# Two more pairs of hidden tiles by seven products, with the weight sums of two pairs made in DRAM

## The chip, the core and the metric

The kernel runs on one core of a Trainium2 chip. The core has five engines with a queue of instructions each: PE (TensorE, matrix products; its weight loads are shown apart as PEld), DVE (VectorE), ACT (ScalarE), POOL (GpSimd) and SP (SyncE, which here only issues transfers). Each engine works its queue in order and waits on semaphores for the others. SBUF holds 128 partitions of working data, PSUM has eight banks of 128x512 float32 for the results of PE, and DRAM holds inputs, output and scratch. The metric is the device time of one execution in microseconds (us). Before the change it was 916.53 us, the median of three runs (915.88 to 916.86).

## What is computed

One layer of a decoder on 512 tokens of width 1024, all in float32: a SwiGLU feed-forward part (FFN), a mixing part (windowed attention next to a state-space scan), a second FFN, each between two RMS norms.

```python
def swiglu(x, w_in, w_out):
    gate, up = jnp.split(x @ w_in, 2, axis=-1)
    return (jax.nn.silu(gate) * up) @ w_out

h = rms_norm(x, ffn1_pre_g[l])
x = x + 0.5 * rms_norm(swiglu(h, ffn1_w_in[l], ffn1_w_out[l]), ffn1_post_g[l])
...
mixed = jnp.concatenate([attn, ssm], axis=-1) @ w_mix_out[l]
x = x + rms_norm(mixed, mix_post_g[l])
h = rms_norm(x, ffn2_pre_g[l])
x = x + 0.5 * rms_norm(swiglu(h, ffn2_w_in[l], ffn2_w_out[l]), ffn2_post_g[l])
```

`w_in` is 1024 x 5632: 22 tiles of 128 columns for the gate and 22 for the up side. The hidden width of 2816 is 22 tiles of 128, counted by f below.

## The kernel before

**Precision.** Every large product is made of three products of a reduced float32 form: an operand is split into a high part (a cast on ACT) and a low part (a subtraction on DVE or POOL), and high x high, high x low and low x high are added in one PSUM bank. `wsplit` (lines 117 and 119) does it for weights, which land in tiles named wraw, wa, wx or wsum and are split into whi and wlo; `split` (lines 163 to 167) does it for activations, named xh and xl, ah and al, bh and bl, tq. All matmuls go through line 144. POOL takes the subtraction where the call says pool=True.

**Order.** The program is written as one sequence and a scheduler puts it into the queues. What is wrapped in `fix` keeps its place in the written order on its engine, and so do all matmuls; the rest is moved about by readiness. Generators ("hooks") hand small pieces of work to the loops of matmuls between two products.

**Standard tiles and pairs.** A tile f of the hidden width takes one product of eight steps for the gate and one for the up side: 2 x 24 matmuls of 512 columns (`products`, the bank is named gu). From some tile on the kernel takes two tiles at once (`pair`), and treats the gate and up sides of the two tiles with the two halves of the inner width (blocks a11, a12, a21, a22) against the four quarters of the activations (b11 to b22) as a 2x2 block product, by Winograd's form of Strassen's scheme: seven products of 24 matmuls with 256 columns, in banks named wx, wy and wq. The price is sums. On the weights' side, per pair, on DVE: c3 = a11 + a21, c2 = c3 + a22, c1 = a21 + a22, c4 = c2 + a12 (line 609). On the activations' side, once: n1, n2, t3, t4. The activations of the pairs are scaled by the norm's reciprocal first (line 533, `scaled`, sixteen instructions of 128x256), then summed and split into seven operands. After the products the gate half is gathered (lines 621 and 638), passed through Silu on ACT (line 639), multiplied with the up half (line 644) and split into ah and al.

**The stages.** First FFN: tiles 0 to 7 standard, then pairs 8 to 20. A `boundary` ends each part: it makes the last output products (yt), adds the residual for half of the tokens at a time (`prep`, lines 317, 319, 166, 167) and starts the next part's first four products step by step behind it (`begin`, the banks are named first). For the second FFN these are tiles 0 and 1. `swiglu_half` then runs tiles 2 to 5 as standard products, with eight transposes of x (`tokens_first`, xt) hooked in between, then the output product of tiles 0 to 5 (`outp(0)`, bank yo), pairs 6, 8 and 10, outp(1), pairs 12, 14 and 16, outp(2), pairs 18 and 20, and `finish`: the last four tiles' output products (yt), the norm and the store. The number of standard tiles is `NSTD = (8, 6)`.

**Buffers.** Weights land in three wraw buffers; a pair's a21 lands in one buffer wa, a22 in two wx, and c1 to c4 take three wsum buffers. A load is issued when its buffer is free, and SP issues in order, so a load that waits holds those behind it.

Of the kernel before, what the change touches and what calls it, by code (L numbers as in the profile page):

```python
# [29 lines left out]
NSTD = (8, 6)  # L30
# [14 lines left out]
class Layer:  # L45
# [30 lines left out]


# [195 lines left out]
    def boundary(self, y, tail, ipost, half, inext, chunks):  # L273
# [40 lines left out]
        def prep(h, k, fix=lambda i: i):  # L314
            t = y(k)[:, hs[h]]
            xk = self.x(k)[:, hs[h]]
            fix(nc.vector.scalar_tensor_tensor(out=t, in0=t, scalar=self.g(ipost, k, half), in1=rr[h],
                                               op0=ALU.mult, op1=ALU.mult))
            fix(nc.vector.tensor_tensor(out=xk, in0=t, in1=xk, op=ALU.add))
            self.split(xh(k)[:, hs[h]], xl(k)[:, hs[h]], xk, self.g(inext, k), fix)  # L320
            self.sq_acc(acc2[:, hs[h]], xk, k == 0, nc.gpsimd)
# [68 lines left out]
    def ffn(self, n, first, scope):  # L390
# [84 lines left out]
        prep = sums(True)  # L475
# [35 lines left out]
    def seven(self, fin, w_in, ig, r, ah, al):  # L511
# [13 lines left out]
        def sums(early=False):  # L525
# [20 lines left out]
            bh, bl = [self.b16(n, F32R) for n in ("bh", "bl")] if early else (None, None)  # L546
            v = lambda t, i: t.rearrange("p (q k) c -> p q (k c)", q=4)[:, i]

            def plain(*ts):
                for t in ts:  # L550
                    i = len(blocks)
                    blocks.append((v(bh, i), v(bl, i)))
                    self.split(*blocks[i], t)

            if early:
                plain(b11)
# [9 lines left out]
            if early:  # L566
                plain(b22, n1)
# [4 lines left out]
            if not early:  # L572
                yield
                bh, bl = [self.b16(n, F32R) for n in ("bh", "bl")]
                plain(b11, b21, b22, n1)
# [11 lines left out]
        def cut(t, pool=False):  # L587
            hi, lo = self.halves(True)
            self.wsplit(t, hi, lo, pool)
            return hi, lo  # L590

        def times(bank, w, xb, first, parted=False):
            for g in range(2):
                for k in range(4):
                    m = slice((4 * g + k) * P, (4 * g + k + 1) * P)
                    st = first and g == 0 and k == 0
                    for i, (wi, xi) in enumerate(((0, 0), (0, 1), (1, 0))):
                        for a, b in ((0, P), (P, HT)) if parted and (g, k, i) == (0, 1, 0) else ((0, HT),):
                            self.mm(bank[:, g * HT + a:g * HT + b], lhsT=w[wi][:, m], rhs=xb[xi][:, k * HT + a:k * HT + b],
                                    start=st and i == 0, stop=g == 1 and k == 3 and i == 2, skip_group_check=True)  # L600
# [6 lines left out]
        def pair(f, lead=False, late=False):  # L607
            (b11, b21, b22, n1), (n2, t3, t4) = blocks, tq
            add = lambda x, z, t: V.tensor_tensor(out=t, in0=x, in1=z, op=ALU.add)
            p2 = lambda t: t.rearrange("p (f c) -> p f c", f=2)  # L610
            half = lambda t, h: t[:, :, h * HT:(h + 1) * HT]
            gt = p2(gp())
            X = self.bank("wx")
            a11 = block(f, 0, 0)
            times(X, cut(a11), b11, True, lead)
            s1 = keep(X)
            a12 = block(f, 0, 1)
            h12 = cut(a12, True)
            Y = self.bank("wy")
            times(Y, h12, b21, True)  # L620
            V.tensor_tensor(out=half(gt, 0), in0=p2(Y), in1=p2(s1), op=ALU.add)
            a21, a22 = block(f, 1, 0), block(f, 1, 1)
            c3 = wsum()
            add(a11, a21, c3)
            c2 = wsum()
            add(c3, a22, c2)
            times(X, cut(c2), n2, False)
            s2 = keep(X)
            c1 = wsum()
            add(a21, a22, c1)  # L630
            Q = self.bank("wq")
            times(Q, cut(c1), n1, True)
            q = keep(Q)
            times(X, cut(c3), t3, False)
# [3 lines left out]
            V.tensor_tensor(out=half(gt, 1), in0=p2(Q), in1=p2(s2), op=ALU.add)
            nc.scalar.activation(out=gt, in_=gt, func=AF.Silu)
            times(X, cut(a22, True), t4, False)  # L640
# [9 lines left out]
        return sums, pair  # L650

    def swiglu_half(self, first, scope):

# [3 lines left out]
        fin = scope.enter_context(self.tc.tile_pool(name="fin", bufs=1))  # L657
        hook = self.tokens_first(fin)
        self.pad(fin, 192)
        o0, _, r, late = first  # L660
        ah, al = self.ktiles("ah", F32R), self.ktiles("al", F32R)
        o = {f: o0[2 * f:2 * f + 2] for f in range(len(o0) // 2)}
        step = lambda: next(hook, None)
        hooks = {(2, 0): {1: step, 3: step, 5: late[0], 7: step}, (2, 1): {0: step, 2: late[1], 4: step, 6: step},
                 (3, 0): {1: step, 3: step, 5: step}, (3, 1): {1: step}}

        def products(f):
            o[f] = []
            for i, c in enumerate((f, NF + f)):
                into = [fin.tile([P, 1024], F32R, name="tq", tag=f"tq2{j}") for j in range(2)] if (f, i) == (2, 0) else None  # L670
                w = self.load(w_in[c], (KD, P), into, pool=i == 1)
                b = self.bank("gu")
                self.mmk(b, w, self.xh, self.xl, hooks=hooks.get((f, i), {}))
                o[f].append(b)

        def hidden(f):
# [3 lines left out]
            V.tensor_tensor(out=ut, in0=o[f][1], in1=r, op=ALU.mult)  # L680
            V.tensor_tensor(out=ut, in0=ut, in1=gt, op=ALU.mult)
            self.split(ah(f % RING), al(f % RING), ut)

        def outp(i):
            f0, nf = FLAST[i]
            for d in range(2):
                b4 = [self.bank("yo") for _ in range(4)]
                for k in range(nf):
# [12 lines left out]
        sums, pair = self.seven(fin, w_in, 4, r, ah, al)  # L701
        for f in range(NSTD[1]):
            if f >= len(o0) // 2:
                products(f)
            if f == 2:
                hidden(0)
                hidden(1)
            if f >= 2:
                hidden(f)
            if f == 3:  # L710
                for _ in hook:
                    pass
                rest = sums()
                for _ in range(7):
                    next(rest)
        next(rest)
# [6 lines left out]
        for f in range(NSTD[1], NF, 2):  # L723
            pair(f, f in (NSTD[1], 12, 18), f == NF - 2)
# [13 lines left out]
        self.finish(fin, y, lambda k: (ah((NF - NT + k) % RING), al((NF - NT + k) % RING)))  # L738

    def finish(self, fin, y, tail):  # L740
# [29 lines left out]
        def gather(b, i):  # L770
            yi = at(y, b, i)
            fx(V.tensor_tensor(out=yi, in0=o[b, i], in1=yi, op=ALU.add))
            fx(nc.scalar.activation(out=self.tmp("sq")[:, :yi.shape[-1]], in_=yi, func=AF.Square,
                                    accum_out=sums[:, b, i:i + 1]))

        def gain(b, i):
# [3 lines left out]
            fx(V.tensor_tensor(out=yg[b, i], in0=at(y, b, i), in1=self.gt[d][:, sl], op=ALU.mult))  # L780
# [644 lines left out]
    def run(self, parts="fmg"):  # L1425
# [4 lines left out]
        first = self.start(chunks, ipre)  # L1430
        for p, q in zip(parts, parts[1:] + " "):
            with ExitStack() as scope:
# [6 lines left out]
                if p != "g":  # L1439
                    first = self.boundary(*out, *post[p], *nxt[q])  # L1440
# [67 lines left out]
```

## Time and profile before

| what | value |
|---|---|
| median of 3 runs | 916.53 us |
| the profiled execution, its own time | 916.19 us |
| its span, first to last instruction | 914.2 us |
| granted clock of PE | 0.998 |
| busy: PE, DVE, ACT, POOL | 898.9, 656.0, 442.0, 217.5 us |
| standard tiles 2 to 5 of the second FFN | 584.72 to 634.36 us of the span |
| outp(0) | 634.36 to 667.16 us |
| pairs 6, 8 and 10 | 667.16 to 724.43 us |
| pairs 8, 10 and 12 of the first FFN | 150.32 to 207.59 us |

A row of the timeline has the start, the length, the engine, the line, the operation, what it writes and reads, how many instructions were merged, and in brackets the idle time before it and what ended it. The end of a matmul is modelled and overlaps the next one's start, so the pace of PE is read from starts. A row of the chain of waits has a start and the time by which that piece took the chain further.

### The profile page before, as it was taken

How to read it: one execution, taken by the hardware profiler on the slowest of the kernel's cores; microseconds unless marked ns; L12 is line 12 of the kernel's file. 1: busy time of each engine (PE TensorE's matmuls, PEld its weight loads, DVE VectorE, ACT ScalarE, POOL GpSimd, SP SyncE). 2: the span in 40 equal slices, each digit the busy share in tenths (PEclk: the TensorE clock that was granted, in tenths of full speed). 3: DMA queues.
4: the chain of work that ended last, by engine and by line, in shares of the span. 5: the costliest groups of instructions: out<-in, count | busy, mean ns of one | idle time of the engine just before them, and what ended most of it. 6: DMA issues, size and time to landing. Idle time of an engine off the chain costs nothing.

```text
span 914.2 us, 15367 instructions
## 1 busy us (share of the span) xinstructions
PE 898.9 (98%) x6169; PEld 801.4 (88%) x6169; DVE 656.0 (72%) x1071; ACT 442.0 (48%) x685; POOL 217.5 (24%) x127
## 2 busy tenths in 40 slices
PE   9999999999999999999999999999999999999996
PEld 7787789998999989978777889888899989998995
DVE  6999786755678666758898567898368557855756
ACT  6263763553355543525745654573355514541542
POOL 0423301322123134500000025523222222221321
PEclk9999999999999999999999999999999999999999
DMA  8223662334231262283321452145222422332222
GB/s 277 94 70 115 196 248 76 107 102 137 77 119 61 68 194 86 92 221 109 116 70 51 153 167 71 29 179 180 97 93 99 133 92 93 116 116 92 92 93 92
DMA packets 47734, 106.81 MB, mean 117 GB/s; under 512 B 7824, under 2 KB 11152, under 8 KB 47120
## 3 DMA queue, kind: packets, MB, share of 16 engines
q1 hardware_dynamic: 46080, 102.21, 34.5%
q10 hardware_dynamic: 1584, 3.63, 1.1%
q8 instruction: 48, 0.79, 0.3%
q14 instruction: 22, 0.18, 0.1%
HBM read 96.13 MB, written 9.70 MB: 116 GB/s over the span
## 4 chain that ended last, share of the span: by engine, by line
PE 79%; DVE 6%; issue 2%; DMA 2%; ACT 1%; POOLq 0%; POOL 0%; DVEq 0%; SPq 0%; ACTq 0%
PE yo L144 21%; PE wx L144 18%; PE wq L144 9%; PE yt L144 6%; PE wy L144 4%; PE gu L144 4%; PE prj L144 4%; PE first L144 3%; PE prv L144 2%; PE mo L144 2%; PE ys L144 1%; PE st L144 1%; DMA w1d<-w1s 1%; PE pt L1098 1%; PE sc L144 1%
## 5 line engine op out<-in xcount | busy, mean ns | idle before, releaser
L117 ACT CAST whi<-wraw 128x1024 fp32r<-128x1024 f32 (+5 forms) x128 | 124.0, 976 | 160.3 <-PE yo L144 65.5
L119 POOL TENSOR_TENSOR wlo<-wraw,whi 128x1024 fp32r<-128x1024 f32 (+1 forms) x41 | 109.2, 2666 | 297.6 <-ACT whi L117 290.3
L119 DVE TENSOR_TENSOR wlo<-wraw,whi 128x1024 fp32r<-128x1024 f32 (+5 forms) x87 | 107.4, 1242 | 75.7 <-ACT whi L117 75.6
L144 PE MATMUL wx<-tq,whi 128*128 128x256 f32 x720 | 124.7, 276 | 0.0
L144 PEld LDWEIGHTS wx<-tq,whi 128*128 128x128 f32 x720 | 108.3, 188 | 0.0
L119 DVE TENSOR_TENSOR wlo<-wsum,whi 128x1024 fp32r<-128x1024 f32 x60 | 73.6, 1227 | 46.5 <-ACT whi L117 46.4
L117 ACT CAST whi<-wsum 128x1024 fp32r<-128x1024 f32 x60 | 63.0, 1050 | 81.8 <-PE yo L144 28.1
L144 PE MATMUL wx<-tq,wlo 128*128 128x256 f32 x360 | 99.4, 276 | 0.0
L119 POOL TENSOR_TENSOR wlo<-wx,whi 128x1024 fp32r<-128x1024 f32 x15 | 41.5, 2764 | 176.3 <-ACT whi L117 128.5
L144 PEld LDWEIGHTS wx<-tq,wlo 128*128 128x128 f32 x360 | 67.6, 188 | 0.0
L144 PE MATMUL gu<-xh,whi 128*128 128x512 f32 x168 | 67.2, 400 | 0.0
L144 PE MATMUL gu<-xh,wlo 128*128 128x512 f32 x168 | 65.7, 391 | 1.1 <-POOL wlo L119 1.1
L144 PE MATMUL wq<-bh,whi 128*128 128x256 f32 x240 | 66.2, 276 | 0.0
L144 PE MATMUL wq<-bl,whi 128*128 128x256 f32 x240 | 66.2, 276 | 0.0
L144 PE MATMUL wq<-bh,wlo 128*128 128x256 f32 x240 | 66.2, 276 | 0.0
L144 PE MATMUL gu<-xl,whi 128*128 128x512 f32 x168 | 65.5, 390 | 0.0
L144 PE MATMUL yo<-ah,whi 128*128 128x512 f32 x144 | 56.3, 391 | 0.0
L144 PE MATMUL yo<-al,whi 128*128 128x512 f32 x144 | 56.1, 389 | 0.0
L144 PE MATMUL yo<-wlo,ah 128*128 128x512 f32 x144 | 56.0, 389 | 0.0
L144 PE MATMUL yo<-whi,ah 128*128 128x512 f32 x144 | 56.0, 389 | 0.0
L144 PE MATMUL yo<-ah,wlo 128*128 128x512 f32 x144 | 56.0, 389 | 0.0
L144 PE MATMUL yo<-whi,al 128*128 128x512 f32 x144 | 56.0, 389 | 0.0
(267 smaller groups left out, 2385.0 us busy)
## 6 DMA issues: line engine op xcount, KB each, us to landing
wraw<-w1i SPq DMA_DIRECT2D x28, 512.0 KB, 3.7
wraw<-w2i SPq DMA_DIRECT2D x28, 512.0 KB, 3.6
wraw<-w2o SPq DMA_DIRECT2D x18, 512.0 KB, 3.7
wraw<-wmi SPq DMA_DIRECT2D x12, 512.0 KB, 4.1
wraw<-w1o SPq DMA_DIRECT2D x8, 512.0 KB, 4.2
wa<-w2i SPq DMA_DIRECT2D x8, 512.0 KB, 3.7
wx<-w2i SPq DMA_DIRECT2D x8, 512.0 KB, 4.0
wa<-w1i SPq DMA_DIRECT2D x7, 512.0 KB, 3.6
```

The lines of the kernel that those rows point to most:

```text
L117: fix(self.nc.scalar.copy(out=hi, in_=raw))
L119: fix(eng.tensor_tensor(out=lo, in0=raw, in1=hi.bitcast(F32), op=ALU.subtract))
L144: i = self.nc.tensor.matmul(*a, **k)
L1098: self.fix(nc.tensor.transpose(b[i][:, o:o + P], sc[:, c:c + P], self.ident))
```

## The change

1. `NSTD` becomes (8, 2): in the second FFN tiles 2 to 5 are the pairs 2 and 4. There are no standard products there any more but those of tiles 0 and 1 in the boundary.
2. For pairs 2 and 4 the sums c1 to c4 are made in DRAM scratch (`block_sums`): each by a plain transfer from SP and an accumulating transfer from POOL, 16 transfers in all, issued step by step between the products of the first FFN's pairs 8, 10, 12 and 14. Pairs 2 and 4 load the finished sums (`whole`). The other pairs still make theirs on DVE; a21 now lands in a wsum buffer and c1 is written over it.
3. The activations' operands of the second FFN's pairs are not scaled by the norm's reciprocal r any more. The parts xh and xl of the boundary serve directly as three of the seven operands; n1, n2, t3 and t4 are made from an unscaled copy gx, which ACT writes in `prep` and from which DVE makes n1 and n2 in the boundary's second half (`wide_sums`). In return the gate half of each pair is multiplied with r before Silu (one DVE instruction of 128x1024 per pair), and the up side's factor is put into `finish` through r4.
4. The first two weight blocks of pair 2 are loaded and split in the boundary (tile ahead). In pair 2 the order on ACT, DVE and SP is pinned.
5. The eight transposes of x move from the standard products to the steps of outp(0). The boundary makes the norm's reciprocal for 512 tokens at once, after pair 2's first product, instead of twice for 256.

```diff
-NSTD = (8, 6)
+NSTD = (8, 2)
+EARLY = (2, 4)
...
+    def block_sums(self):
+        nc, w = self.nc, self.a["w2i"]
+        src = lambda f, up, kh: w[f + NF * up:f + NF * up + 2, :, kh * S:(kh + 1) * S].rearrange("f p c -> p f c")
+        t = self.csum = {(f, c): self.dr.tile([P, 2, S], F32, name=f"c{c}_{f}") for f in EARLY for c in (3, 1, 2, 4)}
+        copy = lambda o, i: self.dma(out=o, in_=i)
+        plus = lambda o, i: self.fix(nc.gpsimd.dma_start(out=o, in_=i, accum_op=ALU.add))
+        make = {"3": lambda f: copy(t[f, 3], src(f, 0, 0)), "+3": lambda f: plus(t[f, 3], src(f, 1, 0)),
+                "1": lambda f: copy(t[f, 1], src(f, 1, 0)), "+1": lambda f: plus(t[f, 1], src(f, 1, 1)),
+                "2": lambda f: copy(t[f, 2], t[f, 3]), "+2": lambda f: plus(t[f, 2], src(f, 1, 1)),
+                "4": lambda f: copy(t[f, 4], t[f, 2]), "+4": lambda f: plus(t[f, 4], src(f, 0, 1))}
+        order = "3a 1a 3b +3a 1b +1a - +3b 2a +1b - 2b +2a - - +2b 4a - +4a - 4b - - +4b"
...
@@ boundary, prep
             self.split(xh(k)[:, hs[h]], xl(k)[:, hs[h]], xk, self.g(inext, k), fix)
+            if wide:
+                fix(nc.scalar.activation(out=t, in_=xk, func=AF.Copy, scale=self.g(inext, k)))
             self.sq_acc(acc2[:, hs[h]], xk, k == 0, nc.gpsimd)
...
             begin(1, k)
-            if k == 3:
+            if wide and k:
+                wide(k - 1)
+            if not wide and k == 3:
                 pre[0][0](fixp=fx)
...
@@ pair
+            if ahead:
+                split = lambda t: cut(t, pin=True)
+                h2, h1 = split(whole(f, 2)), split(whole(f, 1))
+                times(X, ahead[0], blocks[0], True)
+                s1 = keep(X)
+                then(0)
+                then(1)
+                h3 = split(whole(f, 3))
+                Y = self.bank("wy")
+                times(Y, ahead[1], blocks[1], True)
+                then(2)
+                then(3)
+                gate(0, Y, s1)
+                then(4)
+                h4 = split(whole(f, 4))
+                times(X, h2, tq[0], False, True)
+                s2 = keep(X)
+                then(5)
+                h22 = split(block(f, 1, 1))
...
             gate(1, Q, s2)
+            if csum:
+                V.tensor_tensor(out=gt, in0=gt, in1=r.unsqueeze(1).to_broadcast([P, 2, S]), op=ALU.mult)
             nc.scalar.activation(out=gt, in_=gt, func=AF.Silu)
...
+    def wide_sums(self, gx):
...
+            hi, lo = (room[:, kh, i] for i in range(2))
+            self.wsplit(raw, hi, lo)
...
+            if k < 4:
+                V.tensor_tensor(out=h(k, 0), in0=h(k, 0), in1=h(k, 1), op=ALU.subtract)
+            else:
+                V.scalar_tensor_tensor(out=self.n2[:, (k - 4) * HT:(k - 3) * HT], in0=h(k - 4, 0), scalar=-1.0, in1=h(k, 1),
+                                       op0=ALU.mult, op1=ALU.subtract)
...
@@ swiglu_half
+        pair(2, hooks={0: lambda: late[0](fix=self.fix, fixp=self.fix), 1: third, 2: late[1], 3: lambda: put_in(1, 0, 1), 4: fourth,
+                       5: lambda: put_in(2, 1, 0)}, ahead=self.first)
+        hidden(0)
+        hidden(1)
...
+        pair(4)
```

The change moves instructions at three places on which the prediction rests.

**POOL in the first FFN's pairs.** Here wlo<-wx is the low part of a pair's a22 and wlo<-wraw that of the next pair's a12. Before:

```order
L119 TENSOR_TENSOR wlo<-wraw,whi 128x1024
L119 TENSOR_TENSOR wlo<-wx,whi 128x1024
L119 TENSOR_TENSOR wlo<-wraw,whi 128x1024
L119 TENSOR_TENSOR wlo<-wx,whi 128x1024
L119 TENSOR_TENSOR wlo<-wraw,whi 128x1024
```

With the change (c_2 and c_4 are the DRAM sums of pairs 2 and 4):

```order
L139 TENSOR_TENSOR wlo<-wraw,whi 128x1024
L87 DMA c_2_1577<-w2i 256x1x512
L87 DMA c_2_1578<-w2i 256x1x512
L139 TENSOR_TENSOR wlo<-wx,whi 128x1024
L139 TENSOR_TENSOR wlo<-wraw,whi 128x1024
L87 DMA c_4_1581<-w2i 256x1x512
L87 DMA c_4_1582<-w2i 256x1x512
L139 TENSOR_TENSOR wlo<-wx,whi 128x1024
L139 TENSOR_TENSOR wlo<-wraw,whi 128x1024
L87 DMA c_2_1579<-w2i 256x1x512
L87 DMA c_4_1583<-w2i 256x1x512
```

Two accumulating transfers stand behind each a12 and ahead of the same pair's a22; the last two, not shown, stand behind pair 14's a12.

**DVE from the boundary's last steps into the second FFN.** Before, the scaling of all quarters (gp and wx from x) and the norm's reciprocal (nv) stand here around the low parts of tile 2's and 3's weights:

```order
L319 TENSOR_TENSOR x<-ymix,x 128x256
L167 SCALAR_TENSOR_TENSOR xl<-x,sm,xh 128x256
L205 TENSOR_SCALAR nv<-st 128x2
L533 SCALAR_TENSOR_TENSOR gp<-x,sm,rs 128x256 x4
L533 SCALAR_TENSOR_TENSOR wx<-x,sm,rs 128x256
L119 TENSOR_TENSOR wlo<-wraw,whi 128x1024
L533 SCALAR_TENSOR_TENSOR wx<-x,sm,rs 128x256 x3
L205 TENSOR_SCALAR nv<-st 128x2
```

With the change:

```order
L339 TENSOR_TENSOR x<-ymix,x 128x256
L756 SCALAR_TENSOR_TENSOR n_5912<-ymix 128x256
L187 SCALAR_TENSOR_TENSOR xl<-x,sm,xh 128x256
L756 SCALAR_TENSOR_TENSOR n_5912<-ymix 128x256
L184 TENSOR_TENSOR tq<-ymix,tq 128x1024
L184 TENSOR_TENSOR tq<-n_5912,tq 128x1024
L139 TENSOR_TENSOR wlo<-wsum,whi 128x1024 x2
L225 TENSOR_SCALAR nv<-st 128x4
L788 TENSOR_TENSOR ymix<-ymix 128x4x256
L139 TENSOR_TENSOR wlo<-wsum,whi 128x1024
```

The scaling is gone; one of the eight steps of n1 and n2 follows each xl, and two operand splits and two weight splits stand ahead of the reciprocal.

**DVE in the last pair.** Before:

```order
L638 TENSOR_TENSOR gp<-wq,kp 128x2x256
L644 SCALAR_TENSOR_TENSOR gp<-kp,gp 128x2x256
L644 SCALAR_TENSOR_TENSOR gp<-wx,gp 128x2x256
L164 TENSOR_TENSOR al<-gp,ah 128x2x256 x2
L772 TENSOR_TENSOR y<-yt,y 128x512
```

With the change:

```order
L651 TENSOR_TENSOR gp<-wq,kp 128x2x256
L719 TENSOR_TENSOR gp<-gp,rs 128x1024
L726 SCALAR_TENSOR_TENSOR gp<-kp,gp 128x2x256
L726 SCALAR_TENSOR_TENSOR gp<-wx,gp 128x2x256
L184 TENSOR_TENSOR al<-gp,ah 128x2x256 x2
L890 TENSOR_TENSOR y<-yt,y 128x512
```

The multiplication with r stands between the gate's gathering and the step that needs Silu's result; the instructions behind it are the same.

More of the change, by code (lines that the diff above doesn't have):

```diff
@@ L551, in plain @@
                     i = len(blocks)
[L552 to L556, printed above, removed]
+                    b = v(bh, i), v(bl, i)
+                    blocks.append([v4(u) for u in b])
+                    self.split(*b, t)
+            plain(b11)
             V.scalar_tensor_tensor(out=n2, in0=n1, scalar=-1.0, in1=b22, op0=ALU.mult, op1=ALU.subtract)
-            if early:
-                plain(b21)
+            plain(b21)
             yield
@@ L571, in sums, with pairs @@
             self.split(*tq[2], t4)
[L572 to L575, printed above, removed]
             yield
+        return sums, self.pairs(w_in, blocks, tq, wsum, gp, (wsum, wx), r, ah, al)
+    def pairs(self, w_in, blocks, tq, wsum, gp, rooms, r, ah, al, csum=None):
+        nc, V = self.nc, self.nc.vector
+        wa, wx = rooms
         def block(f, up, kh):
             if up:
-                t = wx() if kh else more[0].tile([P, 1024], F32, name="wa", tag="wa")
+                t = wx() if kh else wa()
             else:
@@ L605, in keep, with pair @@
             return t
-        def pair(f, lead=False, late=False):
-            (b11, b21, b22, n1), (n2, t3, t4) = blocks, tq
+        def pair(f, lead=False, late=False, hooks={}, ahead=None):
             add = lambda x, z, t: V.tensor_tensor(out=t, in0=x, in1=z, op=ALU.add)
@@ L611, in pair @@
             half = lambda t, h: t[:, :, h * HT:(h + 1) * HT]
+            then = lambda i: hooks[i]() if i in hooks else None if csum else self.more()
+            four = csum and (f, 2) in csum
             gt = p2(gp())
             X = self.bank("wx")
[L614 to L634, printed above, removed]
@@ L639, in pair @@
+            gate(1, Q, s2)
+            if csum:
+                V.tensor_tensor(out=gt, in0=gt, in1=r.unsqueeze(1).to_broadcast([P, 2, S]), op=ALU.mult)
             nc.scalar.activation(out=gt, in_=gt, func=AF.Silu)
-            times(X, cut(a22, True), t4, False)
+            then(6)
+            times(X, h22 if ahead else cut(a22, True), tq[2], False)
             s = f % RING
@@ L699, in outp @@
                         V.tensor_tensor(out=y(b, d), in0=b4[b], in1=y(b, d), op=ALU.add)
[L701 to L716, printed above, removed]
+        blocks[3] = put(3, part(gx, 0, 0))
+        tq[0] = put(0, n2)
+        wsum = lambda: fin.tile([P, 1024], F32, name="wsum", tag="wsum", bufs=3)
+        pair = self.pairs(w_in, blocks, tq, wsum,
+                          lambda: fin.tile([P, 1024], F32, name="gp", tag="gp"), (wsum, lambda: fin.tile([P, 1024], F32, name="wx", tag="wx", bufs=2)), r, ah, al, self.csum)
+        pair(2, hooks={0: lambda: late[0](fix=self.fix, fixp=self.fix), 1: third, 2: late[1], 3: lambda: put_in(1, 0, 1), 4: fourth,
+                       5: lambda: put_in(2, 1, 0)}, ahead=self.first)
+        hidden(0)
+        hidden(1)
         self.gt = [self.acct() for _ in range(2)]
@@ L722, in swiglu_half @@
         outp(0)
[L723 to L724 removed]
+        for _ in hook:
+            pass
+        for f in range(6, NF, 2):
+            pair(f, f in (6, 12, 18), f == NF - 2)
             if f in (10, 16):
```

158 lines of the change are left out of this document (118 added, 40 removed).

## The prediction

> **What bounds the kernel now.** I read the busy times first, then the shares of the chain of waits.
>
> ```profile
> PE 898.9 (98%) x6169; PEld 801.4 (88%) x6169; DVE 656.0 (72%) x1071; ACT 442.0 (48%) x685; POOL 217.5 (24%) x127
> PE 79%; DVE 6%; issue 2%; DMA 2%; ACT 1%; POOLq 0%; POOL 0%; DVEq 0%; SPq 0%; ACTq 0%
> ```
>
> PE is busy for 898.9 of 914.2 us and holds 79% of the chain. An edit pays where it takes matmuls away or ends a wait of PE; freeing DVE pays nothing by itself. The windows of four stages follow (stretch, its length, busy time and count on PE, PEld, DVE, ACT and POOL, granted clock, DMA share, GB/s).
>
> ```profile
> 584.72:634.36 49.64, 48.44 (x234) 40.00 (x233) 46.22 (x54) 27.84 (x38) 19.01 (x7) 1.00 0.46 159
> 634.36:667.16 32.80, 32.80 (x147) 27.18 (x146) 13.69 (x11) 10.94 (x14) 5.50 (x2) 1.00 0.31 98
> 667.16:724.43 57.27, 57.27 (x507) 57.27 (x506) 39.15 (x39) 31.72 (x37) 15.51 (x6) 1.00 0.31 104
> 150.32:207.59 57.27, 57.27 (x506) 57.27 (x506) 38.91 (x39) 31.03 (x37) 14.96 (x6) 1.00 0.30 96
> ```
>
> The first is the stage that is replaced, tiles 2 to 5: PE lacks 1.20 us, DVE is nearly full (46.22 of 49.64). In outp(0), the second, DVE works 13.69 of 32.80. In three pairs of either FFN (57.27, so 19.09 a pair) PE never idles and the clock is 1.00. The first FFN's pairs matter because the new transfers are issued there.
>
> **The matmuls.** Two pieces of the chain of waits give the pace (start, time, engine, tile, line, matmuls).
>
> ```profile
> 605.93 28.60 PE gu L144 x126
> 667.16 2.87 PE wx L144 x25
> 670.03 2.72 PE wy L144 x24
> ```
>
> A matmul of 512 columns takes 28.60 / 126 = 0.2270 us, one of 256 columns 2.72 / 24 = 0.1133. Tiles 2 to 5 are 8 x 24 = 192 of the first: 43.58. Pairs 2 and 4 are 2 x 7 x 24 = 336 of the second: 38.08. Term A is **-5.50**. One matmul of pair 2 is parted in two, as in the 25-row piece above: 2.87 - 2.72 = **+0.15** (term B).
>
> **The wait that goes.** The timeline around 593 us:
>
> ```profile
> 583.95 6.83 DVE L533 SCALAR_TENSOR_TENSOR gp<-x,sm,rs 128x256 f32<-128x256 f32 x4 [2.56 <-ACT rs L215]
> 585.37 5.12 POOL L119 TENSOR_TENSOR wlo<-wraw,whi 128x1024 fp32r<-128x1024 f32 x2
> 592.03 0.40 PE L144 MATMUL gu<-xh,wlo 128*128 128x512 f32 x1
> 593.42 0.15 DVE L205 TENSOR_SCALAR nv<-st 128x2 f32<-128x2 f32 x1
> 593.63 0.66 PE L505 MATMUL xt<-ident,x 128*128 128x128 f32 x4 [1.20 <-DVE nv L205]
> ```
>
> The product of 592.03 should have been followed 0.227 later, at 592.26; the next matmul starts at 593.63, 1.4 late. The releaser nv stood on DVE behind the scaling, whose four instructions took 6.83 us while POOL made two low parts. This scaling and this place of nv are gone. The sum of the stage agrees: 43.58 + eight transposes + st and rp + 1.4. A transpose is 597.32 to 597.68 with a slower start of the next product (next rows), 0.45; 8 x 0.45 = 3.6; what is left of 49.64 for st and rp is 1.06. So term C is **-1.4**, if nothing takes its place.
>
> ```profile
> 597.32 0.60 PE L505 MATMUL xt<-ident,x 128*128 128x128 f32 x4
> 597.68 0.48 PE L144 MATMUL gu<-xh,whi 128*128 128x512 f32 x1
> ```
>
> What could: nv now stands behind two operand splits and two weight splits (about 1.2 us each, 4.8) after the last xl. Its reader, rp, comes in PE's order after pair 2's second product, 2 x 2.72 = 5.44 after the first four products end. The slack is 5.44 - 4.8, some 0.3 after ACT's part between them; the other operands of pair 2 have more. I take 0, bound 0 to +1.2.
>
> **Transposes moved.** The same eight go to outp(0), 3.6 there and 3.6 less here: **0** (term D), bound 0 to +1, since their results must leave PSUM beside yo's; DVE has 19 us free in that stage, ACT 22.
>
> **Boundary, second half.** DVE now also makes one step of n1 or n2 per step of prep.
>
> ```profile
> 572.25 0.47 DVE L167 SCALAR_TENSOR_TENSOR xl<-x,sm,xh 128x256 fp32r<-128x256 f32 x1
> 572.65 0.41 DVE L319 TENSOR_TENSOR x<-ymix,x 128x256 f32<-128x256 f32 x1
> 572.99 0.48 DVE L167 SCALAR_TENSOR_TENSOR xl<-x,sm,xh 128x256 fp32r<-128x256 f32 x1
> 580.84 0.48 DVE L167 SCALAR_TENSOR_TENSOR xl<-x,sm,xh 128x256 fp32r<-128x256 f32 x1 [0.58 <-ACT xh L166]
> ```
>
> From the first xl to the last, seven steps, it takes (580.84 - 572.25) / 7 = 1.23 a step. The new instruction has two inputs like x<-ymix,x, which takes 572.99 - 572.65 = 0.34. So 1.57 a step, where PE needs 12 x 0.1133 = 1.36 for its four products: PE loses 8 x 0.21 = 1.7 at most, and part of it hides in the lead that DVE has (before, PE waited for xl only at the edges). Against it, one st and one rp fall away, 0.9 of the 1.06 above. ACT's extra copy of 128x256 stands behind its cast, and ACT has room: before its 32 casts xh it waits 19.4 us for DVE (next row).
>
> ```profile
> L166 ACT ACTIVATE xh<-x,sm 128x256 fp32r<-128x256 f32 x32 | 16.2, 506 | 19.4 <-DVE x L319 19.3
> ```
>
> Term E: **+0.2**, bounds -1.1 (all hidden) to +1.4.
>
> **The blocks ahead.** Pair 2's first two blocks are split early in the boundary, in place of tile 2's weights: two casts on ACT and two low parts on DVE, 1.23 each (the size of the 1.21 below), by the order among DVE's additions ymix and acc, around 540 to 545. There DVE waited over 2 us twice for yt; what is left behind can delay the last acc, on which PE's st hangs.
>
> ```profile
> 541.40 0.69 DVE L302 TENSOR_TENSOR ymix<-yt,ymix 128x512 f32<-128x512 f32 x1 [2.11 <-PE yt L144]
> 544.12 0.69 DVE L302 TENSOR_TENSOR ymix<-yt,ymix 128x512 f32<-128x512 f32 x1 [2.03 <-PE yt L144]
> 547.80 0.43 DVE L311 TENSOR_TENSOR acc<-acc,sq 128x256 f32<-128x256 f32 x1 [0.17 <-ACT sq L308]
> 550.72 0.50 PE L144 MATMUL st<-ones,acc 128*128 128x2 f32 x4
> ```
>
> From the last acc's end, 548.23, PE takes 2.49 us until it reaches st in its own order, and two low parts are 2.4: covered, no cost; without the cover it would be 2.4, which lies within the upper end of the range. A pair with sums from DRAM takes seven loads of 512 KB, 3.67 MB in 19.09 us or 192 GB/s; the kernel's first slice and its sixth moved more:
>
> ```profile
> GB/s 277 94 70 115 196 248 76 107 102 137 77 119 61 68 194 86 92 221 109 116 70 51 153 167 71 29 179 180 97 93 99 133 92 93 116 116 92 92 93 92
> ```
>
> I take no cost for them.
>
> **The last pair.** The multiplication with r stands between the gate and Silu. The timeline of the last pair:
>
> ```profile
> 883.41 1.06 ACT L639 ACTIVATE gp<-gp 128x1024 f32<-128x1024 f32 x1 [2.50 <-DVE gp L638]
> 885.24 0.62 ACT L163 CAST ah<-gp 128x512 fp32r<-128x512 f32 x1 [0.76 <-DVE gp L644]
> 886.02 1.46 DVE L164 TENSOR_TENSOR al<-gp,ah 128x512 fp32r<-128x512 f32 x2
> 885.38 13.64 PE yt L144 x60
> L164 DVE TENSOR_TENSOR tq<-wsum,tq 128x1024 fp32r<-128x1024 f32 x6 | 7.2, 1214 | 0.0
> ```
>
> The tail's first six yt matmuls need two older tiles, 6 x 0.227 = 1.36; at 885.38 + 1.36 = 886.74 PE comes to the third. Its ah is ready at 885.86 and its al at about 886.7 now, which is just in time. The new instruction, 128x1024 with two inputs, costs 1.21 by the row of that size, so al comes 1.2 late while ah can be used sooner: **+0.7** (term F), bounds +0.3 to +1.3. In the nine other pairs the product t4 lies between Silu and the use, and DVE is at 39.15 of 57.27: no cost.
>
> **First FFN.** Each of pairs 8, 10, 12 and 14 gets eight small hooks with transfers. On POOL the accumulating ones stand ahead of the pair's a22 (first row each: a12; last: a22).
>
> ```profile
> 140.42 2.44 POOL L119 TENSOR_TENSOR wlo<-wraw,whi 128x1024 fp32r<-128x1024 f32 x1 [30.59 <-ACT whi L117]
> 165.12 2.40 POOL L119 TENSOR_TENSOR wlo<-wraw,whi 128x1024 fp32r<-128x1024 f32 x1 [2.99 <-ACT whi L117]
> 178.78 3.51 POOL L119 TENSOR_TENSOR wlo<-wx,whi 128x1024 fp32r<-128x1024 f32 x1 [11.26 <-ACT whi L117]
> 174.95 2.72 PE wx L144 x24
> 193.99 2.72 PE wx L144 x24
> wraw<-w2i SPq DMA_DIRECT2D x28, 512.0 KB, 3.6
> ```
>
> POOL idles 11.26 us between a pair's a12 and its a22, so issuing there costs nothing. What can cost is SP: the plain copy of c2 reads what the accumulation of c3 writes, so SP waits for it, with the next pair's a21 queued behind. An accumulation reads two blocks and writes one; no row shows one. Bounds: one 512 KB landing, 3.6, and three, 10.8. PE needs c2 of pairs 10 and 12 at 174.95 and 193.99; c3, c2, the cast and the low part on DVE (1.22 + 1.22 + 1.05 + 1.23) and a landing of 3.6 lie ahead, 8.3. So a21 has to leave SP by 166.6 and 185.7. The accumulations that SP waits for start after POOL's a12, at 142.9 and 167.5. They may take 23.7 and 18.2 us; both bounds are below. Term G: **0**, with nothing below it and 2 above in the range. The DRAM traffic, 16 transfers of 512 KB, goes into stages with a DMA share of 0.30.
>
> The sum is -5.50 + 0.15 - 1.4 + 0 + 0.2 + 0.7 + 0 = **-5.85**. The profiled execution took 916.19, so 910.34; the median of the runs shown is 0.34 above it, and the forecast is about 910.5.
>
> **The rivals.**
>
> *Weight loads set the pace (slower).* A 256-column matmul has a weight load each, and PEld is busy for all 57.27 us of the pairs.
>
> ```profile
> L144 PEld LDWEIGHTS wx<-tq,whi 128*128 128x128 f32 x720 | 108.3, 188 | 0.0
> ```
>
> If a new pair went at the 188 ns of this row instead of 113, A would be 336 x 0.188 - 43.58 = +19.6, and the time about 935.6. Against it stands the pace itself: 2.72 for 24 of exactly these matmuls, half of 24 x 0.2270, so the load is hidden. I give it 0.02. [...]
>
> *Slow accumulations hold SP (slower).* Place: SP's copies of c2, ahead of the loads of pairs 12 and 10. It decides from 18.2 us per accumulation. At 25 us pair 12 starts 6.8 late and pair 10 1.3: -5.85 + 8.1, about 918.6; at 30 us 11.8 + 6.3, about 928.5. For it: no row of an accumulation, two transfers follow each other on POOL, and a transfer of half the size, the row below, has taken 8.1. Against: 18.2 is five landings of 512 KB, and a transfer of twice the size took 5.2. Chance 0.08.
>
> ```profile
> um<-ud SPq DMA_DIRECT2D x4, 256.0 KB, 8.1
> w2d<-zb SPq DMA_DIRECT2D x2, 1024.0 KB, 5.2
> ```
>
> [...]
>
> *The second FFN starts starved.* The boundary's DVE steps run slower than 1.57 beside POOL's squares, as the scaling did beside POOL (6.83 us for four), or nv is late at rp. Both bounds together are 1.2 + 1.2 over my terms, with D's bound 3.4: 912 to 914. Chance 0.13.
>
> *More is won.* The boundary's steps hide (-1.3 on E) and the tail costs 0.3: 908.5. Chance 0.07.
>
> **How the numbers follow.** The forecast has 0.70 and by the inner bounds of E and F reaches from 909 to 912. The likeliest time is 910.5. With the gain cases down to 908.0 and the starved start and part of G's bound up to 916.0, about 0.1 is left out above. A change of 0.2% is 1.83 us, about what a measurement of this kernel tells from none: faster is below 914.70, slower above 918.36. The forecast, the starved start up to 914.7 and the larger gain are 0.87 together; the rest of the starved start and a mild hold of SP are 0.04; strong hold and slow loads are 0.09.
>
> **What would show it.** In the chain of waits of the changed kernel: pieces wx, wy, wq with 2.72 per 24 matmuls from about 585 on, and pair 4's end near 38.5 us behind pair 2's start (A, B); outp(0) at about 36.3 us (D); no wait over 1 us on PE for nv or rp, or for xl (C, E); in the tail a wait of about 0.7 for al before the third tile (F); the first FFN's three pairs still at 57.27 and accumulations landing in under 18 us (G). The forecast is wrong if the first FFN's pairs grow, or if the pieces of pairs 2 and 4 exceed 2.72.

## The result, and the profile after

The change made the kernel slower: 927.37 us (median of 6 runs, 923.1 to 930.9) against 916.69 us before (6 runs, 915.88 to 917.62). The ratio is 1.0116, with a 95% interval of 1.0087 to 1.0144. The forecast was 910.5 us, range 908.0 to 916.0. The profiled execution took 929.7 us, its span is 927.9 us.

From the page of the changed kernel, its shares of the chain of waits:

```profile
PE 79%; DVE 12%; DMA 3%; ACT 2%; issue 2%; POOL 1%; SPq 0%; POOLq 0%; DVEq 0%; ACTq 0%
```

DVE's share of the chain went from 6% to 12%. The windows of the changed kernel (columns as in the prediction) say where: pair 8, pair 10, the rest up to pair 12's end, and pair 14.

```profile
150.84:170.00 19.16, 16.62 (x146) 16.42 (x146) 14.01 (x10) 9.13 (x11) 7.76 (x4) 1.00 0.41 123
170.00:193.40 23.40, 19.99 (x169) 19.71 (x169) 18.74 (x16) 10.91 (x12) 7.04 (x5) 0.98 0.60 155
193.40:218.25 24.85, 24.85 (x193) 24.85 (x194) 13.66 (x15) 11.27 (x14) 4.24 (x2) 0.88 0.65 187
250.91:270.01 19.10, 16.47 (x146) 16.27 (x144) 14.56 (x11) 8.65 (x10) 6.05 (x2) 1.00 0.41 117
```

All four rows are stages of the first FFN whose arithmetic the change doesn't touch. PE idles in three of them, and in the one where it doesn't its clock is 0.88. Pairs 8, 10 and 12 took 67.41 us (150.84 to 218.25) in place of 57.27. The second FFN still wins, but less than forecast: the six rows above the last in the next table sum to -1.5 us, where -5.85 was forecast for the whole change. By stages, from the starts on the chains of waits (own_buffer and own_and_tail are experiments below; on the chain a piece starts some 0.16 us behind its first matmul in the timeline, so outp(0) before goes from 634.53 to 667.16 here):

| stage | before | with the change | own_buffer | own_and_tail |
|---|---|---|---|---|
| up to pair 8 | 150.32 | +0.52 | -0.72 | -0.99 |
| pairs 8 to 12 | 57.27 | +10.14 | 0.00 | 0.00 |
| output products, pairs 14 to 20 | 108.97 | +4.54 | +0.01 | 0.00 |
| from there to tile 2 or pair 2 | 268.32 | +0.46 | +1.01 | -0.19 |
| tiles 2 to 5, now pairs 2 and 4 | 49.64 | -9.33 | -9.33 | -9.33 |
| outp(0), now with the transposes | 32.64 | +3.92 | +3.92 | +3.92 |
| pairs 6 to 16 with their output products | 179.87 | 0.00 | +0.01 | 0.00 |
| pairs 18, 20 and the last yt | 51.99 | +2.82 | +2.09 | +0.59 |
| the rest of the span | 15.18 | +0.63 | +0.71 | +0.70 |
| span | 914.2 | 927.9 | 911.9 | 908.9 |

PE's list of waits in the changed kernel has a first line that was not there before (engine, line, what released it: us in total, times, longest):

```profile
PE wx L164 <- DVE kp L710: 9.3, 4, 3.4
```

kp at L710 is the sum of two products on DVE (q = X + q in the pair). PE's last product of the pair goes into the bank X and can start only when DVE has read it. Why kp is late shows in the timeline of DVE, SP and POOL in pair 8 of the changed kernel:

```profile
158.44 1.23 DVE L644 TENSOR_TENSOR wsum<-wraw,wsum 128x1024 f32<-128x1024 f32 x1 [2.44 <-DMA wsum<-w1i]
161.31 4.56 DVE L644 TENSOR_TENSOR wsum<-wsum,wx 128x1024 f32<-128x1024 f32 x2
165.79 3.40 DVE L139 TENSOR_TENSOR wlo<-wraw,whi 128x1024 fp32r<-128x1024 f32 x1
169.12 0.68 DVE L710 TENSOR_TENSOR kp<-wx,kp 128x512 f32<-128x512 f32 x1
150.24 0.52 SPq L160 DMA_DIRECT2D c<-c  x1
150.86 0.52 SPq L614 DMA_DIRECT2D wraw<-w1i  x1
153.03 0.37 SPq L614 DMA_DIRECT2D wsum<-w1i  x1
160.25 3.40 POOL L139 TENSOR_TENSOR wlo<-wx,whi 128x1024 fp32r<-128x1024 f32 x1 [14.44 <-DVE gp L651]
165.64 2.47 POOL L139 TENSOR_TENSOR wlo<-wraw,whi 128x1024 fp32r<-128x1024 f32 x1 [1.98 <-ACT whi L137]
```

The kernel before, in the same pair, a21's load on SP, and c3 and kp on DVE:

```profile
140.64 0.37 SPq L584 DMA_DIRECT2D wa<-w1i  x1
152.52 1.23 DVE L609 TENSOR_TENSOR wsum<-wraw,wa 128x1024 f32<-128x1024 f32 x1
164.17 0.69 DVE L635 TENSOR_TENSOR kp<-wx,kp 128x512 f32<-128x512 f32 x1 [0.59 <-PE wx L144]
```

Three steps follow each other. First, a21 of pair 10 (wsum<-w1i) leaves SP at 153.03. Before, it had a buffer of its own and left at 140.64; now it takes a wsum buffer and waits until the low part of an earlier sum is made. It lands 5.4 us later, while a dependent copy and another load, issued 2 to 3 us earlier (such land in 4.5 and 3.8 us at the median), are still under way. Second, DVE works in order, and the next pair's c3 stands ahead of this pair's kp: DVE waits 2.44 us. Third, what follows on DVE is thereby pushed onto POOL's two low parts: two sums take 4.56 us, a low part 3.40, where such an instruction alone takes 1.22. kp ends at 169.80, and PE starts its last product at 169.85 after 2.54 us of idling.

After two of these waits the clock fell as well. The windows of the changed kernel behind PE's wait of 3.41 us (granted clock is the third figure from the end):

```profile
190.00:193.38 3.38, 0.00 (x0) 0.00 (x1) 3.38 (x4) 1.04 (x1) 2.58 (x3) 0.88 0.31 23
193.38:197.00 3.62, 3.62 (x17) 3.62 (x18) 3.50 (x4) 1.06 (x1) 0.00 (x0) 0.50 1.08 189
197.00:201.90 4.90, 4.90 (x35) 4.90 (x35) 2.78 (x3) 2.05 (x3) 0.00 (x0) 0.75 0.99 321
```

and the chain of waits there and behind the wait of 2.63 us in pair 14:

```profile
193.38 8.55 PE wx L164 x48
270.01 7.35 PE wx L164 x48
```

48 matmuls took 8.55 and 7.35 us in place of 5.44 (behind the second wait the granted clock was 0.50 from 272.0 to 274.0 us), so these two waits cost 3.1 and 1.9 us more than their length. Behind the first wait, of 2.54 us, the granted clock stayed at 1.00 (169.85 to 190.00), but most matmuls up to the next wait started 0.118 us apart in place of 0.113. That cost some 1.1 us more, and no run here shows its cause. With it the sum closes: 2.54 + 1.08 + 3.41 + 3.11 = 10.14 in pairs 8 to 12, and 2.63 + 1.91 = 4.54 in pair 14.

### The profile page after: what moved, and what is told of

Same layout as the page of the kernel before. It is cut to its first block, busy times and chain, and to the rows that moved or that the text cites. A ratio compares the mean times of both kernels' runs of the same rounds, so it can differ in the third digit from the quotient of the medians.

```text
span 927.9 us, 15709 instructions
## 1 busy us (share of the span) xinstructions
PE 903.0 (97%) x6314; PEld 811.2 (87%) x6314; DVE 680.8 (73%) x1069; ACT 455.6 (49%) x705; POOL 220.5 (24%) x132
## 4 chain that ended last, share of the span: by engine, by line
PE 79%; DVE 12%; DMA 3%; ACT 2%; issue 2%; POOL 1%; SPq 0%; POOLq 0%; DVEq 0%; ACTq 0%
PE yo L164 21%; PE wx L164 20%; PE wq L164 9%; PE yt L164 6%; PE wy L164 5%; PE prj L164 4%; PE first L164 3%; DVE wlo L139 2%; PE prv L164 2%; PE gu L164 2%; PE mo L164 2%; DVE pp L959 1%; PE ys L164 1%; PE st L164 1%; DMA w1d<-w1s 1%
## 5 line engine op out<-in xcount | busy, mean ns | idle before, releaser
L139 POOL TENSOR_TENSOR wlo<-wraw,whi 128x1024 fp32r<-128x1024 f32 (+1 forms) x38 | 97.6, 2570 | 287.4 <-ACT whi L137 280.1
L164 PE MATMUL wx<-tq,whi 128*128 128x256 f32 (+1 forms) x817 | 146.5, 282 | 9.3 <-DVE kp L710 9.3
L164 PEld LDWEIGHTS wx<-tq,whi 128*128 128x128 f32 x817 | 126.3, 192 | 10.1 <-DVE kp L710 10.1
L164 PE MATMUL wx<-tq,wlo 128*128 128x256 f32 x408 | 114.8, 281 | 0.0
L644 DVE TENSOR_TENSOR wsum<-wsum,wx 128x1024 f32<-128x1024 f32 x30 | 57.1, 1943 | 0.2
L164 PE MATMUL gu<-xh,wlo 128*128 128x512 f32 x112 | 43.9, 392 | 1.1 <-POOL wlo L139 1.1
L164 PE MATMUL gu<-xh,whi 128*128 128x512 f32 x112 | 44.7, 399 | 0.0
L164 PE MATMUL first<-xl,whi 128*128 128x256 f32 (+1 forms) x144 | 42.8, 297 | 1.2 <-DVE xl L187 1.1
L164 PE MATMUL gu<-xl,whi 128*128 128x512 f32 x112 | 43.6, 390 | 0.0
L164 PE MATMUL first<-xh,whi 128*128 128x256 f32 (+1 forms) x144 | 42.6, 296 | 0.4 <-ACT xh L186 0.4
```

Of the source, the lines that this page charges most:

```text
L139: fix(eng.tensor_tensor(out=lo, in0=raw, in1=hi.bitcast(F32), op=ALU.subtract))
L164: i = self.nc.tensor.matmul(*a, **k)
```

## The experiments

Three theories were open. Theory 1: the shared buffer and the transfers together delay a21, and neither is enough alone. Theory 2: the transfers alone do it (SP held, landings stretched), as the second rival of the prediction said. Theory 3: the buffer alone.

**own_buffer.** a21 of the first FFN has its own buffer again; the sixteen transfers stay.

```diff
-        return sums, self.pairs(w_in, blocks, tq, wsum, gp, (wsum, wx), r, ah, al)
+        wa = lambda: more[0].tile([P, 1024], F32, name="wa", tag="wa")
+        return sums, self.pairs(w_in, blocks, tq, wsum, gp, (wa, wx), r, ah, al)
...
-                    c1 = a21
+                    c1 = a21 if wa is wsum else wsum()
```

> The changed kernel, but in the first FFN a21 has a buffer of its own again (wa) and c1 takes a wsum buffer, as before the change; the transfers that make the sums in DRAM stay. Theory 1 (the shared buffer lets a21's load leave some 10 us later, and the transfers then stretch its landing; neither alone is enough): a21 leaves as in the kernel before, DVE is never held, pairs 8 to 12 come back to 57.3 to 58.5 us and pairs 14 to 20 to 76.3; about 912 to 914 us. Theory 2 (the transfers alone: SP held behind an accumulation and landings stretched): the pairs stay above 62 us and the time above 920. Theory 3 (the buffer alone): as theory 1.

Measured: 913.79 us (912.85 to 913.96), ratio to before 0.9965 (0.9951 to 0.9978). In the timeline of own_buffer, pair 8:

```profile
139.92 0.37 SPq L615 DMA_DIRECT2D wa<-w1i  x1
151.80 1.23 DVE L645 TENSOR_TENSOR wsum<-wraw,wa 128x1024 f32<-128x1024 f32 x1
157.78 1.22 DVE L645 TENSOR_TENSOR wsum<-wa,wx 128x1024 f32<-128x1024 f32 x1
161.64 1.23 DVE L139 TENSOR_TENSOR wlo<-wraw,whi 128x1024 fp32r<-128x1024 f32 x1 [2.63 <-ACT whi L137]
163.46 0.69 DVE L711 TENSOR_TENSOR kp<-wx,kp 128x512 f32<-128x512 f32 x1 [0.59 <-PE wx L164]
159.02 2.40 POOL L139 TENSOR_TENSOR wlo<-wx,whi 128x1024 fp32r<-128x1024 f32 x1 [14.61 <-DVE wsum L645]
```

a21 leaves at 139.92, c3 comes without a wait, and DVE idles while POOL makes a22's low part: no instruction is stretched, and kp waits for PE and not PE for kp. The pairs are back at 57.27 although all transfers run. That excludes theory 2 as a sufficient cause.

**no_dram_sums.** No transfers; pairs 2 and 4 load plain blocks, so the sums are left out of the computation. The shared buffer stays.

```diff
-            nc.sync.dma_start(out=t, in_=csum[f, c].rearrange("p f c -> p (f c)"))
+            src = w_in[f + NF * (c % 2):f + NF * (c % 2) + 2, :, (c // 3) * S:(c // 3 + 1) * S].rearrange("f p c -> p f c")
+            nc.sync.dma_start(out=t.rearrange("p (f c) -> p f c", f=2), in_=src)
...
-        for i in order.split():
+        for i in '- ' * 0:
```

> The changed kernel without the 16 transfers in the first FFN; pairs 2 and 4 load plain weight blocks of the same size in place of the sums, so the sums are left out of the computation. The shared buffer stays. Theory 1: a21 still leaves late, but lands in 3.5 us in place of 5.4 to 6.9, DVE waits under 1 us for it and PE not at all; pairs 8 to 12 about 57.3 to 58, about 912 to 913 us. Theory 2: the same. Theory 3 (the buffer alone): the pairs stay above 62 us, the time above 920.

Measured: 914.51 us (912.72 to 916.7), ratio 0.9977 (0.9967 to 0.9987). Pair 8 in its timeline:

```profile
151.34 0.37 SPq L614 DMA_DIRECT2D wsum<-w1i  x1
155.02 1.23 DVE L645 TENSOR_TENSOR wsum<-wraw,wsum 128x1024 f32<-128x1024 f32 x1 [0.72 <-DMA wsum<-w1i]
157.89 4.58 DVE L645 TENSOR_TENSOR wsum<-wsum,wx 128x1024 f32<-128x1024 f32 x2
162.39 1.21 DVE L139 TENSOR_TENSOR wlo<-wraw,whi 128x1024 fp32r<-128x1024 f32 x1
163.53 0.68 DVE L711 TENSOR_TENSOR kp<-wx,kp 128x512 f32<-128x512 f32 x1
```

a21 leaves as late as with the change (12 us later than in own_buffer, counted in the same stage), but lands in 3.7 us. DVE waits 0.72 us; the two sums still meet POOL (4.58), the low part behind them no longer does (1.21), and kp is in time. That excludes theory 3. The median is 1.5 us above the 912 to 913 expected. The profiled execution is the fastest of the ten; whether PE waits for kp in the slower ones isn't shown.

**neither.** Both edits together; here too the sums are left out of the computation.

> Both of the above: a21 in a buffer of its own, and no transfers for the sums (pairs 2 and 4 load plain blocks, the sums are left out). All theories: pairs 8 to 12 at 57.3, pairs 14 to 20 at 76.3; what is left against the kernel before is the second FFN alone: -5.6 for pairs 2 and 4 with outp(0), +0.8 in the boundary, +0.7 to +2.8 in the last pairs, so 911 to 914 us.

Measured: 913.77 us (912.07 to 915.23), ratio 0.996 (0.9948 to 0.9973). It is as fast as own_buffer: once a21 has its own buffer, the sixteen transfers cost nothing that these runs can tell. Theory 1 stands.

**a22_on_vector.** The low part of a22 is made by DVE, which takes POOL out of the way of the two sums.

```diff
-            times(X, h22 if ahead else cut(a22, True), tq[2], False)
+            times(X, h22 if ahead else cut(a22), tq[2], False)
```

> The changed kernel, but the low part of each pair's a22 (wlo from wx) is made by DVE and not by POOL; everything else, buffer and transfers, as changed. If the late a21 hurts only because it pushes DVE's additions onto POOL's two low parts (c2 and c1 took 4.56 us there for 2.4, the next low part 3.4 for 1.2), DVE reaches kp about 3 us earlier than in the changed kernel although a21 lands as late: PE's waits for kp fall from 2.5 to 3.4 us to under 1, and with them the low clock behind them; 915 to 919 us. If the late landing alone is what PE waits for, the waits stay at 2.5 or grow by 1.2 for the additional instruction, and the time stays above 925.

Measured: 920.55 us (919.9 to 921.17), ratio 1.004 (1.0025 to 1.0055): above the 915 to 919 that the first expectation gave, below the second. Pair 8 and pair 10 in its timeline:

```profile
156.97 1.23 DVE L644 TENSOR_TENSOR wsum<-wraw,wsum 128x1024 f32<-128x1024 f32 x1 [2.68 <-DMA wsum<-w1i]
159.84 2.35 DVE L644 TENSOR_TENSOR wsum<-wsum,wx 128x1024 f32<-128x1024 f32 x2
164.38 0.68 DVE L710 TENSOR_TENSOR kp<-wx,kp 128x512 f32<-128x512 f32 x1
170.14 1.22 DVE L139 TENSOR_TENSOR wlo<-wsum,whi 128x1024 fp32r<-128x1024 f32 x1
181.89 1.22 DVE L644 TENSOR_TENSOR wsum<-wraw,wsum 128x1024 f32<-128x1024 f32 x1 [7.32 <-DMA wsum<-w1i]
166.68 2.13 POOL L87 DMA_DIRECT2D c<-w2i  x2
174.90 0.49 SPq L160 DMA_DIRECT2D c<-c  x1
176.12 0.37 SPq L614 DMA_DIRECT2D wsum<-w1i  x1
```

In pair 8 DVE waits for a21 even longer than with the change (2.68 us), but the two sums take 2.35 us and not 4.56, kp ends at 165.06, and PE doesn't wait: its chain runs on at 2.72 per product. Pair 14 is the same; pairs 14 to 20 are back at 76.3 us. So the landing alone doesn't stop PE there, the collision with POOL is a needed link. In pair 10 another cause shows that the stall of pair 8 had covered. SP's copy of the other c2 waits until 174.90 for an accumulation whose two transfers were issued at 166.68 (8.20 us on the chain), and a21 stands behind it. By the pattern of pair 8, where a21 left as soon as the first low part behind c4 was made, its buffer was free at 171.4. DVE waits 7.32 us, and PE 4.3 us for the low part of a sum, the first line of its list of waits:

```profile
PE wq L164 <- DVE wlo L139: 4.3, 1, 4.3
```

That is the second rival of the prediction, at an accumulation of 8 us and not of 18.

**later_sums.** The shared buffer stays; each accumulation stands behind a22 on POOL, the dependent copies come a pair later, and the transfers reach to pair 18.

```diff
-        order = "3a 1a 3b +3a 1b +1a - +3b 2a +1b - 2b +2a - - +2b 4a - +4a - 4b - - +4b"
+        order = "3a 1a 3b 1b - - +3a,+1a - - - - 2a - +3b,+1b - - - - 2b - +2a - - - - 4a - +2b - - - - 4b - +4a - - - - - - +4b"
...
             times(X, h22 if ahead else cut(a22, True), tq[2], False)
+            then(7)
```

> The changed kernel with its shared buffer, but each accumulating transfer stands on POOL behind the pair's a22 (in place of behind its a12), and the plain copies that depend on one come a pair later; the same 16 transfers, now spread over pairs 8 to 18. If it is the coincidence that costs (the accumulations run just when the next pair's a21 is to land, and SP waits for them ahead of it): a21 lands in under 4.5 us in pair 8, DVE waits under 1 us for it, no wait of PE for kp over 1 us, pairs 8 to 12 at 57.3 to 59 and pairs 14 to 20 at 76.3 us, about 913 to 916 us. If the transfers cost wherever they stand, because of their traffic: a stall of 2 to 3 us with low clock behind it in most pairs that have one, and above 920 us.

Measured: 921.64 us (919.16 to 923.16), ratio 1.0056 (1.0039 to 1.0074). Neither expectation held as a whole. Pairs 8, 12 and 14 are at full pace; in pairs 10 and 16 the chain is 2.8 and 2.4 us late, and the others that have transfers are not. In pair 16 the accumulation had ended, since the copy waits for it; there was only that plain copy and a load. The last two rows are pair 14:

```profile
261.72 0.47 SPq L160 DMA_DIRECT2D c<-c  x1
263.23 0.37 SPq L614 DMA_DIRECT2D wraw<-w1i  x1
264.93 0.37 SPq L614 DMA_DIRECT2D wsum<-w1i  x1
269.80 1.22 DVE L644 TENSOR_TENSOR wsum<-wraw,wsum 128x1024 f32<-128x1024 f32 x1 [1.69 <-DMA wsum<-w1i]
276.57 3.42 DVE L139 TENSOR_TENSOR wlo<-wraw,whi 128x1024 fp32r<-128x1024 f32 x1
280.64 5.73 PE wx L164 x48
249.48 1.23 DVE L644 TENSOR_TENSOR wsum<-wraw,wsum 128x1024 f32<-128x1024 f32 x1 [1.69 <-DMA wsum<-w1i]
256.84 1.21 DVE L139 TENSOR_TENSOR wlo<-wraw,whi 128x1024 fp32r<-128x1024 f32 x1
```

In pair 16 a21 lands in 4.8 us, with a copy and a load just ahead of it; DVE waits 1.69 us, and the low part meets POOL (3.42). In pair 14 DVE waits just as long, and nothing is lost (1.21). So the length of DVE's wait doesn't decide. What goes with the price is which low part starts first: DVE's of a11 or POOL's of a12. In pairs 8, 10 and 16 of no_dram_sums and 14 of later_sums DVE's starts first, by 0.41 to 1.56 us, and takes 1.21; kp is at most 0.1 late. In pairs 8 and 14 of the changed kernel and 10 and 16 of later_sums POOL's starts first, by 0.04 to 0.41 us, and DVE's takes 3.39 to 3.42; PE waits 2.4 to 2.8 us. No pair here lies in between. Another place for the transfers doesn't cure that; a buffer of its own for a21 does. Behind PE's wait of 2.79 us in pair 10 here the granted clock stayed at 1.00 (187.90 to 194.00) and 48 matmuls took 5.72; behind that of 2.44 us in pair 16 they took 5.73. Behind the 2.63 us of the changed kernel the clock fell to 0.50.

**own_and_tail.** own_buffer, and in the second FFN the last pair's gate is multiplied with r in two halves, the first right behind the first gate product; pair 18's a22 has its low part from DVE.

```diff
-            gate = lambda h, u, s: V.tensor_tensor(out=half(gt, h), in0=p2(u), in1=p2(s), op=ALU.add)
+            def gate(h, u, s):
+                V.tensor_tensor(out=half(gt, h), in0=p2(u), in1=p2(s), op=ALU.add)
+                if csum and late:
+                    V.tensor_tensor(out=half(gt, h), in0=half(gt, h),
+                                    in1=r[:, h * HT:(h + 1) * HT].unsqueeze(1).to_broadcast([P, 2, HT]), op=ALU.mult)
...
-            if csum:
+            if csum and not late:
...
-            times(X, h22 if ahead else cut(a22, True), tq[2], False)
+            times(X, h22 if ahead else cut(a22, not (csum and lead and f > 12)), tq[2], False)
```

> The kernel of own_buffer with two edits in the second FFN: in the last pair the gate is multiplied with r in two halves, the first one right behind the first gate product, so that 128x512 and not 128x1024 stand ahead of the last Silu; and the low part of a22 of pair 18 is made by DVE, not by POOL. Expected from own_buffer: the wait of the tail for ah (0.41) goes, and the wait for kp in pair 18 (0.97, with 0.3 of slower matmuls behind it) goes: 913.8 - 1.4 to 1.7, about 912.2 us, which is faster than both kernels. If the two waits only shift to other instructions, 913.5 to 914.

Measured: 911.88 us (910.8 to 913.03), ratio 0.9944 (0.9932 to 0.9956): faster than both kernels, 5.0 us below before. The waits that it removes, from PE's list of waits in own_buffer:

```profile
PE wx L164 <- DVE kp L711: 1.0, 1, 1.0
PE yt L164 <- ACT ah L183: 0.4, 1, 0.4
```

and the tail's yt on the chain of own_and_tail:

```profile
878.89 14.13 PE yt L164 x60
```

In own_buffer PE waits 0.97 us for kp in pair 18 and 0.41 us for ah ahead of the third tile's yt; in own_and_tail neither wait is there, and the sixty yt run in one piece.

## Why the prediction was wrong

**The step that failed is term G**, the first FFN at 0 with at most 2 us above. It measured +14.7 us (10.14 and 4.54) in the profiled execution, and 0.0 with a21 in its own buffer (own_buffer). Three things in it were wrong.

- The deadline. I took the moment at which PE needs c2 of the next pair, and found 18.2 and 23.7 us of room for an accumulation. The deadline that counts is DVE's: c3 of the next pair stands on DVE ahead of this pair's kp, so a late a21 delays the present pair. The order of DVE on which this rests could be read from the kernel before (c3 at 152.52, kp at 164.17 in its timeline).
- The buffer. The change put a21 into the ring of the sums. I wrote it down as a part of the change and gave it no price. It moves a21's load from 140.64 to 153.03, which alone is harmless (no_dram_sums), but leaves no lead: DVE's waits for a21 of up to 1.23 us cost at most 0.1 us there, and those of 2.06 and more cost PE 2.5 us and more wherever POOL makes a22's low part.
- The traffic. I let the DRAM traffic go into stages with a DMA share of 0.30. a21's median landing was 5.3 us in place of 3.6, as the DMA issues of the changed kernel show (sums, first loads, accumulations):

```profile
wsum<-w1i SPq DMA_DIRECT2D x7, 512.0 KB, 5.3
c<-w2i POOLq DMA_DIRECT2D x8, 512.0 KB, 7.6
```

The accumulation itself lay inside my bounds of 3.6 to 10.8 us at its median; the longest took 12.1.

The rival "slow accumulations hold SP" had the queue right, but it isn't what the changed kernel paid for. There a21 of pair 10 left when its buffer came free (the low part ends at 153.00), 2.8 us behind the copy that had waited for an accumulation, and ahead of a21 of pair 12 SP waited last for another low part (175.21), not for the copy (174.71). Only in a22_on_vector did an accumulation hold a21, and there 8.2 us were enough and not 18.2; that threshold was wrong by the same deadline. That the rival's 928.5 us, for accumulations of 30 us, lies near the measured 927.37 is luck: the longest took 12.1.

**Terms A and B** held: in the chain of the changed kernel the products of pairs 2 and 4 go at 2.72 per 24 matmuls but for the first two (2.88 and 2.98, for which no run shows the cause), and the rival of the weight loads falls with them. **Term C** held: PE waits neither for nv nor at rp in the second FFN. **Term D** measured +0.3 beside the moved 3.6 (outp(0) +3.92). **Term E** was mis-sized: the stretch up to pair 2 came out at -0.19 to +1.01 in three traces where +0.2 was forecast, but the st and rp that I let fall away there only moved into pair 2 with twice the work. Two chain pieces of own_buffer:

```profile
588.06 0.79 PE st L164 x8
591.82 0.89 PE rp L164 x8
```

1.68 us stand there in place of the 1.06 that the prediction found for st and rp in the stage before. That is 0.6 of the 1.0 by which pairs 2 and 4 (-9.33) fell short of the forecast (-5.50 + 0.15 - 1.4 - 3.6 = -10.35); the other 0.4 is in the first two products. **Term F** was right for what it spoke of, 0.41 where 0.7 was taken, but pair 18 was missing. POOL has a tail weight to split there, but so it had before the change (856.47 in its timeline), and PE didn't wait. New is the shared buffer, which own_buffer takes back in the first FFN only. In pair 18 of own_buffer DVE waits 0.83 us for a21, two sums take 4.56, and the low part meets POOL again:

```profile
855.28 3.42 DVE L139 TENSOR_TENSOR wlo<-wraw,whi 128x1024 fp32r<-128x1024 f32 x1
```

There kp came 0.97 us late, and with the slower matmuls behind it (5.73 for 48 in place of 5.44) the last pairs cost 2.09 in own_buffer and 2.82 with the change. own_and_tail ends this by taking work off POOL; a buffer of its own for a21 in the second FFN was not tried, so the buffer's part in pair 18 is argued and not shown. What `finish` has to do more (a scale in the square, r4 in the gain) was not priced at all; behind the last yt the span is 0.6 to 0.7 longer.

With a21 in its own buffer the time was 913.8 us, 3.3 above the forecast: 1.0 in pairs 2 and 4, 1.4 from pair 18 and the tail beyond F, 0.7 behind the last yt, and 0.2 that is less than what the start of the program differs from run to run (pair 8 started at 149.14 to 151.32 in these traces).

**The spread.** The changed kernel's runs lie 7.8 us apart, those of before 1.7. In the changed kernel a wait of PE of 2.63 us was followed by half the clock for a while (0.50 from 272.0 to 274.0 us, 7.35 for 48 matmuls) and one of 2.54 us was not (1.00); in later_sums waits of 2.79 and 2.44 us were not (5.72 and 5.73). So waits of nearly the same length had different prices; what decides between them no run here shows. That this is what spreads the runs was not tested.

## What to carry to other kernels

When a load is made later, look for the first instruction that reads it on an engine that works in order, and then at everything that stands behind that instruction, however unrelated: that, and not the reader's own consumer, is the deadline. A buffer that is merged into another ring is a change of a load's start time and belongs into the sum with a price; transfers that are harmless beside a load that lands some 8 us ahead of its reader (own_buffer, pair 8: it leaves at 139.92, lands in 3.6 at the median and is read at 151.80) cost 15 us beside the same load without that lead.

## What was not expected of the hardware

- A landing that came 2.4 us late grew on its way: DVE's two additions beside POOL's subtraction took 4.56 us in place of the 2.35 with none beside them (a22_on_vector), the low part behind them 3.40 for 1.22, and half the clock behind PE's wait (granted 0.50) then cost 1.9 and 3.1 us more. Why DVE and POOL slow each other is not shown.
- An accumulating transfer of 512 KB in DRAM took 7.6 us (median, 6.4 to 12.1), where a plain load of 512 KB lands in 3.6; sixteen transfers of that size in the pairs cost nothing that these runs can tell where a21 was loaded ahead (913.79 with, 913.77 without).
